# Eight experts' feed-forward on one core: the stores of seven experts regrouped into 8 KB runs

## The chip, the core and the metric

The kernel runs on one NeuronCore of a Trainium2 chip. The metric is the device time of one execution in microseconds (us): 180.81 us, the median of 4 runs between 180.52 and 181.08 us. One further execution was taken with the hardware profiler; it took 181.58 us, and all rows of the profile come from it.

## The reference

Eight experts each have their own 256 tokens of 512 values and their own two weight matrices. All arrays are float32.

```python
n_experts, capacity, hidden, expert_hidden = 8, 256, 512, 2048
# x (8, 256, 512), w1 (8, 512, 2048), w2 (8, 2048, 512)
h = np.matmul(x, w1)
h = np.maximum(h, 0)
return np.matmul(h, w2).astype(np.float32)     # (8, 256, 512)
```

## The kernel before

Data comes in through one queue of GpSimd (POOL), queue q0 of the profile, which also casts float32 to bfloat16 on the way. Ahead of it SyncE (SP) loads a first quarter of x, `x_head`, on its own queue q1. Then q0 carries, in the order of the code: the rest of x; w1 and w2 of experts 0 and 1; w1 and w2 of experts 2 and 3; w1 of 4 and 5; w2 of 4; w2 of 5; w1 and w2 of 6; w1 of 7; w2 of 7 in two halves. The list `loads` holds the twelve weight loads. Four slots of SBUF (`w1_sb`, `w2_sb`, `NS = 4`) hold weights, so a load waits until the expert that used its slot four places earlier is done. x is put in slot 2 of `w2_sb` first, so the load of w2 of experts 2 and 3 also waits until x has been transposed.

TensorE (PE) first transposes x in a loop of four rounds. Each round fills two PSUM tiles, `xt_ps`, which VectorE (DVE) and ScalarE (ACT) copy to `xT` (`copy_xt`, line 194). Then a loop runs over the eight experts: 64 matmuls into `h_ps`, with the ReLU on ACT (line 225, into `hT`), and 32 matmuls into two tiles `o_ps` of 128 tokens each. DVE copies these into `out_sb` (line 211); of the last expert ACT copies the second (line 231). Semaphores `c_w1` and `c_w2`, which SP raises as each load lands (line 138), let PE go on; `c_o` tells PE that an `o_ps` tile has been copied away, and PE waits for it at the last hidden matmul of each half of the next expert.

Every partition of `out_sb` holds two neighbouring tokens of each expert. Thus a partition's piece of an expert is 4 KB that is contiguous in the output too. Experts 0 to 6 go out with one DMA from POOL (line 187, called "the bulk store" below). It follows the last load in q0. A tiny store of 16 times 64 bytes (line 175) stands in the queue between the two halves of w2 of expert 7, and the bulk store is not issued before it has landed:

```python
pool.wait_ge(s_event, 4)        # DVE has copied expert 6
pool.wait_ge(d_pool, 32)        # x and the tiny store have landed
pool.dma_start(
    out_v[:, :E - 1, :], out_sb[:, :E - 1].rearrange("p e m h -> p e (m h)")
).then_inc(d_pool, 16)
```

The last expert's 512 KB go out with a DMA from SP on q1 (line 140, "the last store"), after the last two copies of `o_ps`. At the end POOL waits for the bulk store and then for the last store, and the engines meet at a barrier.

In this kernel each weight slot has a semaphore of its own, so POOL may issue as many loads ahead as there are free slots.

Of the kernel before, what the change touches and what calls it, by code (L numbers as in the profile page):

```python
# [8 lines left out]
FP32 = mybir.dt.float32  # L9
# [7 lines left out]
def kernel(  # L17
# [8 lines left out]
    P = 128  # L26
    E, C, H = x.shape
    F = w1.shape[2]
    MC = C // P
# [3 lines left out]
    R = E * C // P  # L33

    HEAD = 4

    NS = 4
# [8 lines left out]

    x_v = x.rearrange("e (pp r) k -> (e pp) (r k)", r=R)
    w1_v = w1.rearrange("e (p ko) n -> p e (ko n)", ko=K1)  # L50
    w2_v = w2.rearrange("e (p h j) n -> p e h (j n)", h=2, j=JH)
    out_v = out.rearrange("e (p mo) k -> p e (mo k)", mo=MC)


    places, free = {}, FIRST_FREE
# [1 line left out]
    def allot(name, shape, dtype):  # L57
        nonlocal free
        places[name] = free
        t = nc.alloc_sbuf_tensor_at(name, shape, dtype, offset=free)  # L60
        free += math.prod(shape[1:]) * mybir.dt.size(dtype)
        return t


    out_sb = allot("out_sb", [P, E, MC, H], FP32)
    w1_sb = allot("w1_sb", [P, NS, K1 * F], BF16)
    w2_sb = allot("w2_sb", [P, NS, K2 * H], BF16)
    xT = allot("xT", [P, K1, MC, E * P], BF16)
# [4 lines left out]
    x_sb = w2_sb[:, 2, :]  # L73
    X_AT = W2_AT + 2 * K2 * H * 2

    xt_ps = [nc.alloc_psum_tensor(f"xt_ps{i}", [P, R // MC, P], BF16) for i in range(MC)]
    h_ps = [nc.alloc_psum_tensor(f"h_ps{i}", [P, GJ * C], FP32) for i in range(UG)]
    o_ps = [nc.alloc_psum_tensor(f"o_ps{i}", [P, H], FP32) for i in range(MC)]

    def sem(name):  # L80
        return tc.alloc_semaphore(name)

    d_w = {
        (w, i): sem(f"d_w{w}_{i}")
        for w, slots in [(1, (0, 2, 3)), (2, (0, 1, 2, 3))]
        for i in slots
    }
    d_half, d_pool, d_last = sem("d_half"), sem("d_pool"), sem("d_last")  # L90


    s_event = sem("s_event")
    s_pe, v_last = sem("s_pe"), sem("v_last")

    def after_transposes(n):
        return s_pe, n

    def after_hidden(e, groups):
        return s_pe, K1 * MC + e * (NG + MC) + groups  # L100

    def after_outputs(e, halves):
        return s_pe, K1 * MC + e * (NG + MC) + NG + halves
# [10 lines left out]
    loads = []  # L114
# [3 lines left out]
    for e in range(6, E - 1):  # L118
        loads += [(1, (e,), 0, 2), (2, (e,), 0, 2)]
    loads += [(1, (E - 1,), 0, 2), (2, (E - 1,), 0, 1), (2, (E - 1,), 1, 1)]  # L120
    landed, counts = [], {}
    for w, es, h, _ in loads:
        s = d_half if h else d_w[w, es[0] % NS]
        counts[id(s)] = counts.get(id(s), 0) + 16
        landed.append((s, counts[id(s)]))

# [4 lines left out]
    with tc.tile_critical(no_gpsimd_drain=True):  # L133

        sp = nc.sync
        for i, (w, es, h, n) in enumerate(loads):
            sp.wait_ge(*landed[i])
            sp.sem_inc((c_w1, c_w2)[w - 1], n * len(es) if w == 2 else len(es))
        sp.wait_ge(v_last, MC)
        sp.dma_start(  # L140
            out_v[:, E - 1, :], out_sb[:, E - 1].rearrange("p m h -> p (m h)")
        ).then_inc(d_last, 16)


        pool = nc.gpsimd
        pool.dma_start(x_sb[:, HEAD * H:], x_v[:, HEAD * H:]).then_inc(d_pool, 16)  # L146
        pool.memset(identity[:], 0.0).then_inc(s_event)  # L147
        pool.wait_ge(s_event, 1)

# [1 line left out]
            out=identity[:],  # L151
# [7 lines left out]
        for i, (w, es, h, n) in enumerate(loads):  # L159


            old = es[-1] - NS
            if w == 2 and 2 in es:
                tc.wait_critical_data_deps()
                pool.wait_ge(*after_transposes(K1 * MC))
            if old >= 0 and h == 0:
                if w == 1:
                    pool.wait_ge(*after_hidden(old, NG))
                else:
                    pool.wait_ge(*after_outputs(old, MC))  # L170
            if i == len(loads) - 1:


                pool.wait_ge(s_event, 3)
                pool.dma_start(  # L175
                    out_v[:16, 0, :16], out_sb[:16, 0, 0, :16]
                ).then_inc(d_pool, 16)
            e, ne, at_slot = es[0], len(es), es[0] % NS
            if w == 2:
                src = w2_v[:, e:e + ne, h:h + n, :].rearrange("p e h n -> p e (h n)")  # L180
                dst = w2_sb[:, at_slot:at_slot + ne, h * JH * H:(h + n) * JH * H]
            else:
                src, dst = w1_v[:, e:e + ne, :], w1_sb[:, at_slot:at_slot + ne, :]
            pool.dma_start(dst, src).then_inc(landed[i][0], 16)  # L184
        pool.wait_ge(s_event, 4)
        pool.wait_ge(d_pool, 32)
        pool.dma_start(  # L187
            out_v[:, :E - 1, :], out_sb[:, :E - 1].rearrange("p e m h -> p e (m h)")
        ).then_inc(d_pool, 16)

        def copy_xt(copy, ko, m):
            return copy(  # L194
                xT[:, ko, m].rearrange("k (ep r2) -> k ep r2", r2=R // MC),
                xt_ps[m][:].rearrange("k r2 ep -> k ep r2"),
            )


        dve = nc.vector  # L200
        dve.sem_inc(c_xt[0], 1)
        for ko in range(K1):
            dve.wait_ge(*after_transposes(ko * MC + 1))
            copy_xt(dve.tensor_copy, ko, 0).then_inc(c_xt[0])
        dve.sem_inc(c_o, MC)
        for e in range(E):
            for m in range(MC):
                if e == E - 1 and m == 1:
                    break
                dve.wait_ge(*after_outputs(e, m + 1))  # L210
                cp = dve.tensor_copy(out_sb[:, e, m, :], o_ps[m][:])  # L211
                cp.then_inc(v_last if e == E - 1 else c_o)
            if e in (4, E - 2):
                dve.drain().then_inc(s_event)  # L214


        act = nc.scalar
        act.sem_inc(c_xt[1], 1)
        for ko in range(K1):
            act.wait_ge(*after_transposes(ko * MC + 2))  # L220
            copy_xt(act.copy, ko, 1).then_inc(c_xt[1])
# [6 lines left out]
                    mybir.ActivationFunctionType.Relu,  # L228
                ).then_inc(c_h)
        act.wait_ge(*after_outputs(E - 1, MC))  # L230
        act.copy(out_sb[:, E - 1, 1, :], o_ps[1][:]).then_inc(v_last)  # L231

# [1 line left out]
        pe = nc.tensor  # L236
# [45 lines left out]
        def last_column(step):  # L282

            return (P - 1) * step * 2
# [25 lines left out]
                t.then_inc(s_pe)  # L310

        pe.wait_ge(s_event, 2)
        pe.wait_ge(d_pool, 16)
        x_first = X_AT + last_column(K1)
        pe.reg_mov(reg["x"], x_first)
        loop("transposes", reg["x"], x_first + K1 * 2, transposes)
# [116 lines left out]


        pool.drain()
        pool.wait_ge(d_pool, 48).then_inc(s_event)
        pool.wait_ge(d_last, 16).then_inc(s_event)


# [28 lines left out]
```

## Time and profile before

| what | value |
|---|---|
| median of 4 runs | 180.81 us (180.52 to 181.08) |
| the profiled execution: time, span | 181.58 us, 179.8 us |
| PE, ACT, DVE, POOL busy | 127.1, 38.7, 15.8, 10.2 us |
| q0: packets, bytes, share of the 16 DMA engines' span | 3456, 38.80 MB, 96.8% |
| q1: the same | 288, 1.57 MB, 2.3% |
| HBM read and written | 71.30 MB, 4.20 MB |
| bulk store: size, issue, time from issue to landing | 3584 KB, 164.63 us, 12.9 us |
| last store: the same | 512 KB, 175.59 us, 3.2 us |
| first and last wait of SP for a load (line 138) passed at | 33.1 us, 168.8 us |

The span runs from the first to the last instruction; the time of the execution is longer by 1.8 us that lie around it. The bytes of a queue are counted at the destination, where a weight has 2 bytes; 4 bytes of it are read. A "DMA share" is the mean busy share of the core's 16 DMA engines.

### The profile page before, as it was taken

What the parts mean: (1) busy time and instruction counts of PE and PEld (TensorE: products, weight loads), DVE (VectorE), ACT (ScalarE), POOL (GpSimd) and SP (SyncE); (2) the same over time, 40 slices, a digit from 0 to 9 for tenths busy, and PEclk for the clock granted to TensorE, in tenths of its full rate; (3) what the DMA queues carried; (4) which work ended last, traced back from release to release, by engine and by line L of the source; (5) the groups of instructions that cost most, each with busy time, mean ns of one, the idle gap of its engine ahead of it and who ended that gap; (6) DMA issues with size and microseconds to landing.
All of it is one profiled execution on the core that took longest, in us unless ns stands there. A gap on an engine that the chain in (4) does not pass through costs nothing. (4 is left out here: it accounts for less than half of the span.)

```text
span 179.8 us, 2088 instructions
## 1 busy us (share of the span) xinstructions
PE 127.1 (71%) x824; PEld 89.9 (50%) x832; DVE 15.8 (9%) x20; ACT 38.7 (21%) x38; POOL 10.2 (6%) x21
## 2 busy tenths in 40 slices
PE   0006630593029999994069999999999999869990
PEld 0006530493013696594024884894794695349630
DVE  0202520000000200110000200200200200200010
ACT  0202420044000044044000260242052063004400
POOL 6100010000000002001000100100100000002000
PEclk9999999999756999999759999999999999978999
DMA  5998999999899999989999998999999899899994
GB/s 213 236 236 186 233 230 197 215 233 230 179 233 233 197 211 233 230 179 233 233 200 208 233 230 179 233 233 200 208 233 230 179 233 233 184 222 206 379 420 167
DMA packets 3744, 40.37 MB, mean 225 GB/s; under 512 B 288, under 2 KB 288, under 8 KB 1312
## 3 DMA queue, kind: packets, MB, share of 16 engines
q0 software_dynamic: 3456, 38.80, 96.8%
q1 hardware_dynamic: 288, 1.57, 2.3%
HBM read 71.30 MB, written 4.20 MB: 420 GB/s over the span
## 5 line engine op out<-in xcount | busy, mean ns | idle before, releaser
L264 PE MATMUL o_ps<-w_sb,hT 128*128 x248 | 59.6, 395 | 19.5 <-PEq L239 18.7
L264 PE MATMUL h_ps<-xT,w_sb 128*128 x512 | 61.5, 282 | 11.8 <-PEq L239 11.8
L264 PEld LDWEIGHTS h_ps<-xT,w_sb 128*128 x512 | 58.1, 146 | 16.1 <-issue 12.7
L225 ACT ACTIVATE hT<-h_ps 128x1024 bf16<-128x1024 f32 x32 | 32.7, 1023 | 111.2 <-PE h_ps L264 111.2
L264 PEld LDWEIGHTS o_ps<-w_sb,hT 128*128 128x128 bf16 x256 | 25.4, 101 | 51.1 <-issue 24.6
L211 DVE COPY out_sb<-o_ps 128x512 f32<-128x512 f32 x15 | 9.7, 686 | 141.2 <-PE o_ps L264 141.2
L264 PE MATMUL xt_ps<-identity,w_sb 128*128 128x128 bf16 x64 | 7.6, 312 | 16.5 <-PEq L239 16.5
L264 PEld LDWEIGHTS xt_ps<-identity,w_sb 128*128 x64 | 6.5, 147 | 17.3 <-issue 17.3
L184 POOL DMA_DIRECT2D w_sb<-in_w_dram x12 | 7.4, 616 | 105.5 <-PE h_ps L264 57.4
L194 ACT COPY xT<-xt_ps 128x1024 bf16<-128x1024 bf16 x4 | 4.0, 1012 | 12.8 <-PE xt_ps L264 12.8
L194 DVE COPY xT<-xt_ps 128x1024 bf16<-128x1024 bf16 x4 | 4.9, 1224 | 12.8 <-PE xt_ps L264 12.8
L187 POOL DMA_DIRECT2D out_dram<-out_sb x1 | 1.0, 962 | 33.9 <-DMA out_dram<-out_sb 33.9
L194 ACT ACT_TABLE_LOAD x1 | 1.3, 1283 | 7.0 <-DVE w_sb L132 7.0
L231 ACT COPY out_sb<-o_ps 128x512 f32<-128x512 f32 x1 | 0.6, 585 | 5.9 <-PE o_ps L264 5.9
L132 DVE CAST w_sb<-x_head 128x2048 bf16<-128x2048 f32 x1 | 1.2, 1228 | 5.6 <-DMA x_head<-in_x_dram 5.6
L175 POOL DMA_DIRECT2D out_dram<-out_sb x1 | 0.5, 509 | 14.7 <-DVEq L214 14.7
L146 POOL DMA_DIRECT2D w_sb<-in_x_dram x1 | 0.7, 679 | 0.8 <-POOLq L452 0.8
L150 POOL TENSOR_SCALAR_AFFINE_SELECT identity<-identity 128x128 bf16<-128x128 bf16 x1 | 0.3, 283 | 0.2 <-POOL identity L147 0.2
L147 POOL MEMSET identity<- 128x128 bf16 x1 | 0.2, 223 | 0.0
L452 POOL MEMSET const-float32-0.0<- 128x1 f32 x1 | 0.1, 93 | 0.2 <-issue 0.2
L452 POOL MEMSET const-bfloat16-1.0<- 128x1 bf16 x1 | 0.1, 95 | 0.0
L452 POOL MEMSET const-uint8-127<- 128x1 uint8 x1 | 0.1, 95 | 0.0
(1 smaller groups left out, 0.1 us busy)
## 6 DMA issues: line engine op xcount, KB each, us to landing
w_sb<-in_w_dram POOLq DMA_DIRECT2D x5, 4096.0 KB, 48.9
w_sb<-in_w_dram POOLq DMA_DIRECT2D x5, 2048.0 KB, 51.5
out_dram<-out_sb POOLq DMA_DIRECT2D x1, 3584.0 KB, 12.9
w_sb<-in_w_dram POOLq DMA_DIRECT2D x2, 1024.0 KB, 44.1
w_sb<-in_x_dram POOLq DMA_DIRECT2D x1, 1536.0 KB, 12.5
x_head<-in_x_dram SPq DMA_DIRECT2D x1, 1024.0 KB, 4.8
out_dram<-out_sb SPq DMA_DIRECT2D x1, 512.0 KB, 3.2
out_dram<-out_sb POOLq DMA_DIRECT2D x1, 1.0 KB, 34.4
```

What stands on the lines that cost most here:

```text
L132: nc.vector.tensor_copy(x_sb[:, :HEAD * H], x_head[:])
L146: pool.dma_start(x_sb[:, HEAD * H:], x_v[:, HEAD * H:]).then_inc(d_pool, 16)
L150: pool.affine_select(out=identity[:], in_=identity[:], compare_op=mybir.AluOpType.not_equal, fill=1.0, base=0, pattern=[[-1, P]], channel_ ...
L175: pool.dma_start(out_v[:16, 0, :16], out_sb[:16, 0, 0, :16]).then_inc(d_pool, 16)
L184: pool.dma_start(dst, src).then_inc(landed[i][0], 16)
L187: pool.dma_start(out_v[:, :E - 1, :], out_sb[:, :E - 1].rearrange("p e m h -> p e (m h)")).then_inc(d_pool, 16)
L194: return copy(xT[:, ko, m].rearrange("k (ep r2) -> k ep r2", r2=R // MC), xt_ps[m][:].rearrange("k r2 ep -> k ep r2"),)
L211: cp = dve.tensor_copy(out_sb[:, e, m, :], o_ps[m][:])
L225: act.activation(hT[:, g * GJ:(g + 1) * GJ, :].rearrange("p a c -> p (a c)"), h_ps[g % UG][:], mybir.ActivationFunctionType.Relu,).then_in ...
L231: act.copy(out_sb[:, E - 1, 1, :], o_ps[1][:]).then_inc(v_last)
L264: return pe.add_instruction(inst)
L452: nc = _bacc.Bacc("TRN2", target_bir_lowering=False, num_devices=1)
```

## The change

The rows of the first six experts are dealt to partitions anew, so that a partition holds four neighbouring tokens of one expert: experts 2i and 2i+1 share tile i, the even one on partitions 0 to 63, the odd one on 64 to 127, and a run of 8 KB is contiguous in `out_sb` and in the output. Expert 6 keeps its 4 KB runs and lies with expert 7 in a new tile `last_sb`.

- The bulk store becomes two: three pairs in 8 KB runs (3 MB), issued once expert 5 has been copied and the tiny store has landed, then expert 6 (512 KB).
- The tiny store covers 16 partitions of experts 0, 2 and 4: 48 pieces of 64 bytes in place of 16.
- `copy_xt` makes three copies in place of one, eight times in all.
- The copies of `o_ps` for experts 0 to 5 become two of 64 partitions each, in place of one of 128.
- POOL's DMAs take three semaphores in turn (`d_pool`), and DMA i waits until DMA i-3 has landed, so at most three are under way.

```diff
-    out_v = out.rearrange("e (p mo) k -> p e (mo k)", mo=MC)
+    HP = P // 2
+    PAIRS = E // 2 - 1
+    out_pairs = out[:2 * PAIRS].rearrange("(i s) (q r) k -> s q i (r k)", s=2, r=2 * MC)
+    out_v = out.rearrange("e (p m) k -> p e (m k)", m=MC)
...
-    out_sb = allot("out_sb", [P, E, MC, H], FP32)
+    out_sb = allot("out_sb", [P, PAIRS, 2 * MC, H], FP32)
+    last_sb = allot("last_sb", [P, 2, MC, H], FP32)
...
-    d_half, d_pool, d_last = sem("d_half"), sem("d_pool"), sem("d_last")
+    d_pool, d_last = [sem(f"d_pool{i}") for i in range(3)], sem("d_last")
...
+    of_load = [i + 1 for i in range(len(loads) - 1)] + [len(loads) + 1]
+    small, bulk, bulk2 = len(loads), len(loads) + 2, len(loads) + 3
+
+    def landed(i):
+        return d_pool[i % 3], 16 * (i // 3 + 1)
...
+        def queue(i, dst, src):
+            if i >= 3:
+                pool.wait_ge(*landed(i - 3))
+            pool.dma_start(dst, src).then_inc(d_pool[i % 3], 16)
...
-                pool.dma_start(
-                    out_v[:16, 0, :16], out_sb[:16, 0, 0, :16]
-                ).then_inc(d_pool, 16)
+                queue(small, out_pairs[0, :16, :, :16], out_sb[:16, :, 0, :16])
...
-            pool.dma_start(dst, src).then_inc(landed[i][0], 16)
+            queue(of_load[i], dst, src)
+        pool.wait_ge(*landed(small))
         pool.wait_ge(s_event, 4)
-        pool.wait_ge(d_pool, 32)
-        pool.dma_start(
-            out_v[:, :E - 1, :], out_sb[:, :E - 1].rearrange("p e m h -> p e (m h)")
-        ).then_inc(d_pool, 16)
+        queue(bulk, out_pairs, out_sb[:].rearrange("p i r h -> p i (r h)"))
+        pool.wait_ge(s_event, 5)
+        queue(bulk2, out_v[:, E - 2, :], last_sb[:, 0].rearrange("p m h -> p (m h)"))
...
         def copy_xt(copy, ko, m):
+            EP = 2 * PAIRS
+            for t in range(2):
+                copy(
+                    xT[:, ko, m, :EP * P].rearrange(
+                        "k (e t pp r4) -> k t e pp r4", e=EP, t=2, r4=R // 4
+                    )[:, t],
+                    xt_ps[m][:, :, :EP * (P // E)].rearrange(
+                        "k (r4 t) (e pp) -> k t e pp r4", t=2, e=EP
+                    )[:, t],
+                )
             return copy(
...
+        def copy_out(copy, e, m):
+            if e >= 2 * PAIRS:
+                return copy(last_sb[:, e - 2 * PAIRS, m, :], o_ps[m][:])
+            i, s = divmod(e, 2)
+            for t in range(2):
+                inst = copy(
+                    out_sb[s * HP:(s + 1) * HP, i, t * MC + m, :],
+                    o_ps[m][t * HP:(t + 1) * HP, :],
+                )
+            return inst
...
-            if e in (4, E - 2):
+            if e in (4, E - 3, E - 2):
                 dve.drain().then_inc(s_event)
...
-        pool.wait_ge(d_pool, 48).then_inc(s_event)
+        for i in (bulk, bulk2):
+            pool.wait_ge(*landed(i)).then_inc(s_event)
```

More of the change, by code (lines that the diff above doesn't have):

```diff
@@ L81, in sem @@
         return tc.alloc_semaphore(name)
[L85 to L89, printed above, removed]
-    d_half, d_pool, d_last = sem("d_half"), sem("d_pool"), sem("d_last")
+    d_pool, d_last = [sem(f"d_pool{i}") for i in range(3)], sem("d_last")
     s_event = sem("s_event")
@@ L120 @@
     loads += [(1, (E - 1,), 0, 2), (2, (E - 1,), 0, 1), (2, (E - 1,), 1, 1)]
[L121 to L125, printed above, removed]
+    of_load = [i + 1 for i in range(len(loads) - 1)] + [len(loads) + 1]
+    small, bulk, bulk2 = len(loads), len(loads) + 2, len(loads) + 3
+    def landed(i):
+        return d_pool[i % 3], 16 * (i // 3 + 1)
     x_pool = ctx.enter_context(tc.tile_pool(name="x_pool", bufs=1))
@@ L136 @@
         for i, (w, es, h, n) in enumerate(loads):
-            sp.wait_ge(*landed[i])
+            sp.wait_ge(*landed(of_load[i]))
             sp.sem_inc((c_w1, c_w2)[w - 1], n * len(es) if w == 2 else len(es))
@@ L140 @@
         sp.dma_start(
-            out_v[:, E - 1, :], out_sb[:, E - 1].rearrange("p m h -> p (m h)")
+            out_v[:, E - 1, :], last_sb[:, 1].rearrange("p m h -> p (m h)")
         ).then_inc(d_last, 16)
         pool = nc.gpsimd
-        pool.dma_start(x_sb[:, HEAD * H:], x_v[:, HEAD * H:]).then_inc(d_pool, 16)
+        def queue(i, dst, src):
+            if i >= 3:
+                pool.wait_ge(*landed(i - 3))
+            pool.dma_start(dst, src).then_inc(d_pool[i % 3], 16)
+        queue(0, x_sb[:, HEAD * H:], x_v[:, HEAD * H:])
         pool.memset(identity[:], 0.0).then_inc(s_event)
@@ L183 @@
                 src, dst = w1_v[:, e:e + ne, :], w1_sb[:, at_slot:at_slot + ne, :]
-            pool.dma_start(dst, src).then_inc(landed[i][0], 16)
+            queue(of_load[i], dst, src)
+        pool.wait_ge(*landed(small))
         pool.wait_ge(s_event, 4)
-        pool.wait_ge(d_pool, 32)
-        pool.dma_start(
-            out_v[:, :E - 1, :], out_sb[:, :E - 1].rearrange("p e m h -> p e (m h)")
-        ).then_inc(d_pool, 16)
+        queue(bulk, out_pairs, out_sb[:].rearrange("p i r h -> p i (r h)"))
+        pool.wait_ge(s_event, 5)
+        queue(bulk2, out_v[:, E - 2, :], last_sb[:, 0].rearrange("p m h -> p (m h)"))
         def copy_xt(copy, ko, m):
+            EP = 2 * PAIRS
[8 more added lines that the diff above has]
+                )
             return copy(
-                xT[:, ko, m].rearrange("k (ep r2) -> k ep r2", r2=R // MC),
-                xt_ps[m][:].rearrange("k r2 ep -> k ep r2"),
-            )
+                xT[:, ko, m, EP * P:].rearrange("k (ep r2) -> k ep r2", r2=R // MC),
+                xt_ps[m][:, :, EP * (P // E):].rearrange("k r2 ep -> k ep r2"),
+            )
+        def copy_out(copy, e, m):
[8 more added lines that the diff above has]
+            return inst
         dve = nc.vector
@@ L210 @@
                 dve.wait_ge(*after_outputs(e, m + 1))
-                cp = dve.tensor_copy(out_sb[:, e, m, :], o_ps[m][:])
+                cp = copy_out(dve.tensor_copy, e, m)
                 cp.then_inc(v_last if e == E - 1 else c_o)
-            if e in (4, E - 2):
+            if e in (4, E - 3, E - 2):
                 dve.drain().then_inc(s_event)
@@ L230 @@
         act.wait_ge(*after_outputs(E - 1, MC))
-        act.copy(out_sb[:, E - 1, 1, :], o_ps[1][:]).then_inc(v_last)
+        copy_out(act.copy, E - 1, 1).then_inc(v_last)
         pe = nc.tensor
@@ L312 @@
         pe.wait_ge(s_event, 2)
-        pe.wait_ge(d_pool, 16)
+        pe.wait_ge(*landed(0))
         x_first = X_AT + last_column(K1)
```

## Prediction

> **What bounds the kernel now.** I read the table of engine DMA use first, then the chain that ended last, then the stretches at the end, then the waits of SP and POOL.
>
> ```profile
> DMA  5998999999899999989999998999999899899994
> q0 software_dynamic: 3456, 38.80, 96.8%
> q1 hardware_dynamic: 288, 1.57, 2.3%
> ```
>
> The 16 DMA engines are occupied for 96.8 + 2.3 = 99% of the span. No engine of the core comes near (PE 71%).
>
> ```profile
> 159.09 0.04 issue
> 159.13 8.86 PE h_ps L264 x64
> 167.99 0.26 PE o_ps L264
> 168.25 0.05 issue
> 168.30 6.65 PE o_ps L264 x30
> 174.96 0.02 issue
> 174.98 0.58 ACT out_sb L231
> ```
>
> In the chain of waits the last expert starts at 159.1, when w1 of expert 7 has landed (SP passes that wait at 159.0), and runs unbroken into the last store. This looks like a bound by PE. The stretches of the end, whose last columns are DMA share and GB/s, say more:
>
> ```profile
> 100.00:150.00 50.00, 49.73 (x352) 37.43 (x355) 5.01 (x8) 15.92 (x16) 2.64 (x5) 1.00 1.01 216
> 168.00:175.00 7.00, 6.89 (x31) 2.93 (x30) 0.24 (x1) 1.04 (x2) 0.00 (x0) 1.00 1.02 419
> 176.00:177.00 1.00, 0.00 (x0) 0.00 (x0) 0.00 (x0) 0.00 (x0) 0.00 (x0) 1.00 0.62 254
> 177.00:178.00 1.00, 0.00 (x0) 0.00 (x0) 0.00 (x0) 0.00 (x0) 0.00 (x0) 1.00 0.72 291
> 178.00:179.00 1.00, 0.00 (x0) 0.00 (x0) 0.00 (x0) 0.00 (x0) 0.00 (x0) 1.00 0.02 8
> ```
>
> The bulk store runs at 419 GB/s with every DMA engine busy until about 176, and in the last microsecond 8 GB/s are left: one engine alone still works. The trace's packet and landing records show it. On every load one of the 16 engines reports about 1 us after the rest: for w1 of experts 0 and 1 the first fourteen by 31.93, the fifteenth at 32.15, the last at 33.12. I call it the straggler. It ends its share of the bulk store at 177.14, only then starts its eight packets of the last store (the others began theirs at 176.43), ends them at 178.39, and this landing at 178.74 is the last event before the closing barrier. So the end is set by the total work of one DMA engine that is never idle; PE's chain has 177.14 - 176.43 = 0.71 us of slack against it.
>
> Where the straggler fell behind is in the records too: its first packet of x begins about 0.5 us after it finished `x_head`, while the others follow within 6 ns, and takes 1.804 us in place of 0.926. No other packet after 5 us is longer than its kind by more than 0.12 us.
>
> **The time base.** The profiled execution took 181.58 (span 179.8, 1.78 around it), 0.77 above the median of 180.81. I sum on the profiled one and carry the difference over to the median. What a measurement here can tell from no change is about 0.3%, 0.54 us.
>
> **8 KB runs.** In the bulk store 4 KB packets of one engine start every 155.5 ns. Packets of 8 KB exist in the trace only as the `x_head` load, in the other direction: every 306 ns. An engine now has 56 x 155.5 = 8.71 us of bulk store; after, 24 x 306 + 8 x 155.5 = 8.59. That is -0.12 us, all of it on the straggler and so on the end. Bounds for an 8 KB store packet: 301 ns, if it had no cost beyond the bytes that the 16 KB reads show (605.5 ns, hence about 150 per 4 KB), which gives -0.24; twice the 172 ns of the slowest kind of 4 KB packet, the first of each engine, which gives 24 x 33 ns = +0.79. I take 306: same size, same 16 engines. [...]
>
> **The tiny store.** Its packets take 24 ns, one per engine; now three, so +0.05 us, ahead of the second half of w2 of expert 7 and the bulk store. If they do not follow each other so closely, I bound it by the 0.18 us between the landing of the load before it (163.87) and its own (164.05). **The second bulk store** adds a completion record of 9 to 22 ns per engine: +0.02. It is issued beside the first's 7 us of transfer; a POOL issue takes 0.5 to 0.7 us.
>
> **Three DMAs in flight.** POOL now issues each DMA when the third before it has landed; behind a waiting POOL stand only its own later DMAs. SP's waits show landings at 33.1, 52.5, 71.9, 91.2, 110.5, 120.2, 130.0, 139.6, 149.3, 159.0, 163.9, 168.8. Example: w2 of expert 5 was issued at 76.3, now at about 91.8, but w1 of 4 and 5 and w2 of 4 lie ahead of it until 120. The tightest place is the second half of w2 of expert 7: issued at 130.1 before, now after the landing at 159.0. POOL needs 0.28 to 0.6 us from semaphore to issue and 0.55 for the issue, so 160.2. From the end of an issue to a first packet at most 1.35 us passed (bulk store: issue over at 165.59, first packet at 166.94, and that one followed a busy queue). So 161.5 at the latest, and the fastest engines finish the first half at 162.06, the straggler a microsecond later. No gap, 0.5 us to spare: 0. The bulk store itself waits for the same landing at 164.05 as before.
>
> **Copies.** 512 elements take DVE 690 ns, 1024 take 1224: 156 ns fixed, so three copies in place of one are +0.31 us; ACT alike (585, 1012). Four rounds: +1.3 us, or +2.5 if both engines' shares add up, and the transposes end at 25.7 to 26.9 in place of 24.4. The first hidden matmul waits for weights until 33.1, so this is covered by 6 us; w2 of experts 2 and 3, which waits for the transposes, has a queue filled until 52 ahead of it. The halved output copies: two of 690 ns for one, 1.38 us until the first `c_o` and 2.76 until the second. PE asks for them at the last matmul of each half, some 3.6 and 7.2 us after the outputs end: covered. Expert 6 keeps single copies and is done at 157.6. All 0; without cover each transfer of `o_ps` would cost 0.7 us, and even that only beyond the 0.71 us of slack.
>
> **Sum.** -0.12 + 0.05 + 0.02 = -0.05: 181.53 on the profiled execution, 180.76 on the median. I write 180.7.
>
> **Rivals.**
>
> *Faster: the straggler catches up.* Its 1.4 us are lost around 4.8 to 7.1, just as POOL has finished issuing three weight loads (2.81 to 4.99) on top of x. After the change the third of them, w1 of 2 and 3, waits until x has landed at 13.8. [...] The fifteenth engine then decides, 33.12 - 32.15 = 0.97 us earlier: 180.76 - 0.97 = 179.8. Half of that stays within 0.3%. Against it: the later issues of loads, from 24.4 to 130.1, caused no such stall, and nothing proves the cause. [...]
>
> *Slower: late issue itself stalls an engine.* [...] If the straggler loses there what it lost on x, 0.5 + 0.88 = 1.4 us, the end moves fully: 182.1. If another engine does, 1.4 - 0.97 = 0.4: 181.2. [...] Against it: the bulk store before was issued 2.3 us before its first packets and no packet but one (+28 ns) was long. The 344 ns bound of the 8 KB packets would end at 181.6.
>
> *The runs are cut to 4 KB again:* then nothing remains but +0.07, 180.9, within 0.3%. *PE late by over 0.71 us:* nothing found that would do it.
>
> **How the numbers follow.** Little changed 0.47, the straggler catching up by over 0.54 us 0.33, a stall at the late issue or slow 8 KB writes 0.20. The range reaches to 179.5 on the fast side, which takes in that rival with its 8 KB bound, and to 181.7 on the slow side, leaving out the full stall. For the likeliest case alone it is 180.3 to 181.2.
>
> **What would show it.** Right: POOL's line for the 8 KB store near 164.6, SP's last landing at 168.8 to 168.9, 425 to 430 GB/s while the 8 KB packets run, the last landing at 178.6 to 178.7, transposes over by 27. The fast rival: SP's first load wait passes near 32.2 in place of 33.1 and every later one too. The slow rival: the last load lands after 169.5, or GB/s falls between 161 and 164. I am wrong altogether if PE stops for `c_o`, or if a stretch of the middle falls below 216 GB/s.

## The result and the profile after

The changed kernel takes 180.92 us (median of 50 runs), the kernel before 180.57 us (74 runs); the ratio is 1.002 with a 95% interval of 1.0013 to 1.0026. So it is slower by 0.36 us. That is inside the 0.3% that the prediction called no change and inside its range, but the sum said -0.05 us and the interval excludes that: a small loss where a smaller gain was forecast.

Time and span must be read apart here. In 63 executions of the changed kernel the time is 1.95 us or more above the span, 2.00 us in the mean; in the 149 of the kernel before that ran beside the experiments it is 1.71 to 1.82 us, 1.76 in the mean. The mean span is 179.00 against 178.85 us. So 0.24 us of the loss lie outside the span, where the prediction did not look, and 0.1 to 0.15 us inside it (0.15 by the mean spans, 0.12 by the medians of the time).

The profiled execution of before on which the prediction rests was an odd one: 181.58 us, when 74 runs lie between 180.31 and 181.53. A second trace of the same kernel (the run e1_before below, 180.68 us) has no DMA engine that lands 1 us late: w1 of experts 0 and 1 lands by 32.17 us on fifteen engines and at 32.24 on the last. SP's waits for the loads, with their first and last start in us, show it. Of that second trace of before:

```profile
L138 SPq EVENT_SEMAPHORE  x1: 17/17/17, 32.3 to 32.3; - x1
L138 SPq EVENT_SEMAPHORE  x2: 17/17/17, 163.0 to 167.9; - x2
```

And of the changed kernel, where the line has become 143:

```profile
L143 SPq EVENT_SEMAPHORE  x1: 17/17/17, 32.2 to 32.2; - x1
L143 SPq EVENT_SEMAPHORE  x2: 17/17/17, 162.9 to 168.4; - x2
```

The loads run alike until 163; then the last one, the second half of w2 of expert 7, lands 0.5 us later than in the second trace of before. The chain of the changed kernel, cut at its ends, is the one of before, some 0.9 us earlier only because the straggler is missing:

```profile
158.12 0.04 issue
158.16 8.96 PE h_ps L295 x64
...
174.12 0.59 ACT last_sb L221
```

The windows of time at the end (window, PE, PEld, DVE, ACT, POOL, clock, DMA share, GB/s), first of the second trace of before:

```profile
100.00:150.00 50.00, 50.00 (x353) 37.06 (x352) 4.30 (x7) 16.38 (x16) 2.26 (x5) 1.00 1.01 215
168.00:175.00 7.00, 6.05 (x29) 2.55 (x26) 0.69 (x1) 0.74 (x2) 0.00 (x0) 1.00 1.02 422
177.00:178.00 1.00, 0.00 (x0) 0.00 (x0) 0.00 (x0) 0.00 (x0) 0.00 (x0) 1.00 0.10 37
178.00:179.00 1.00, 0.00 (x0) 0.00 (x0) 0.00 (x0) 0.00 (x0) 0.00 (x0) 1.00 0.00 0
```

Then of the changed kernel:

```profile
100.00:150.00 50.00, 49.55 (x346) 36.68 (x349) 9.75 (x15) 16.39 (x16) 2.67 (x5) 1.00 1.01 215
168.00:174.00 6.00, 6.00 (x29) 2.55 (x26) 0.10 (x1) 0.19 (x1) 0.00 (x0) 1.00 1.01 429
177.00:178.00 1.00, 0.00 (x0) 0.00 (x0) 0.00 (x0) 0.00 (x0) 0.00 (x0) 1.00 0.25 98
178.00:179.00 1.00, 0.00 (x0) 0.00 (x0) 0.00 (x0) 0.00 (x0) 0.00 (x0) 0.83 0.00 0
```

The middle is the same (215 GB/s in both, where the first trace of before had 216), the 8 KB packets move 429 GB/s in place of 422, and yet more is left to move after 177 (98 against 37). What was gained by the stores was lost before they began. The window from 163 to 167.3, in which the last load's packets run, shows where, of the second trace of before:

```profile
163.00:167.30 4.30, 4.30 (x40) 4.08 (x39) 0.00 (x0) 2.21 (x3) 0.96 (x1) 1.00 0.96 209
```

and of the changed kernel:

```profile
163.00:167.30 4.30, 4.30 (x38) 3.95 (x38) 0.00 (x0) 2.19 (x3) 1.34 (x2) 1.00 0.98 194
```

The DMA engines are as busy (0.96, 0.98) and move less. The packet records say how: in the changed kernel 21 of the last load's packets, between 165.18 and 166.38 us, take 684 to 1004 ns in place of 625, together 4.85 us or 303 ns per DMA engine. In the second trace of before it is 7 ns per engine. I call this the stretch: what the packets of the last load take above 625 ns each, divided by 16.

### The profile page after: what moved, and what is told of

It is laid out like the page before. It is cut to its first block, busy times and chain, and to the rows that moved or that the text cites. A ratio compares the mean times of both kernels' runs of the same rounds, so it can differ in the third digit from the quotient of the medians.

```text
span 179.2 us, 2129 instructions
## 1 busy us (share of the span) xinstructions
PE 126.7 (71%) x824; PEld 89.7 (50%) x832; DVE 25.2 (14%) x40; ACT 39.2 (22%) x46; POOL 10.6 (6%) x22
## 5 line engine op out<-in xcount | busy, mean ns | idle before, releaser
L224 DVE COPY out_sb<-o_ps 64x512 f32<-64x512 f32 x24 | 16.5, 689 | 103.2 <-PE o_ps L295 102.8
L206 ACT COPY xT<-xt_ps 128x384 bf16<-128x384 bf16 x8 | 3.4, 482 | 11.9 <-PE xt_ps L295 11.9
L221 DVE COPY last_sb<-o_ps 128x512 f32<-128x512 f32 x3 | 2.0, 688 | 28.9 <-PE o_ps L295 28.9
L206 DVE COPY xT<-xt_ps 128x384 bf16<-128x384 bf16 x8 | 4.1, 552 | 12.0 <-PE xt_ps L295 12.0
L221 ACT COPY last_sb<-o_ps 128x512 f32<-128x512 f32 x1 | 0.6, 586 | 5.9 <-PE o_ps L295 5.9
L214 DVE COPY xT<-xt_ps 128x256 bf16<-128x256 bf16 x4 | 1.7, 414 | 0.0
L214 ACT COPY xT<-xt_ps 128x256 bf16<-128x256 bf16 x4 | 1.6, 390 | 0.0
L155 POOL DMA_DIRECT2D out_dram<-last_sb x1 | 0.6, 574 | 0.0
```

The lines of the kernel that those rows point to most:

```text
L155: pool.dma_start(dst, src).then_inc(d_pool[i % 3], 16)
L206: copy(xT[:, ko, m, :EP * P].rearrange("k (e t pp r4) -> k t e pp r4", e=EP, t=2, r4=R // 4)[:, t], xt_ps[m][:, :, :EP * (P // E)].rearran ...
L214: return copy(xT[:, ko, m, EP * P:].rearrange("k (ep r2) -> k ep r2", r2=R // MC), xt_ps[m][:, :, EP * (P // E):].rearrange("k r2 ep -> k ...
L221: return copy(last_sb[:, e - 2 * PAIRS, m, :], o_ps[m][:])
L224: inst = copy(out_sb[s * HP:(s + 1) * HP, i, t * MC + m, :], o_ps[m][t * HP:(t + 1) * HP, :],)
```

## The experiments

Two questions: what lies outside the span, and what stretches the last load. Time, mean span, mean of time minus span, and the stretch per engine in the profiled execution of each kernel:

| kernel | time us | ratio (interval) | span | outside | stretch ns |
|---|---|---|---|---|---|
| e1_before | 180.60 | 1.0002 (0.9993 to 1.0011) | 178.87 | 1.76 | 7 |
| e1_after | 180.93 | 1.0018 (1.0009 to 1.0027) | 178.89 | 2.02 | 354 |
| e1_queue3 | 180.51 | 0.9996 (0.9987 to 1.0005) | 178.75 | 1.79 | 39 |
| e1_layout | 180.88 | 1.0016 (1.0007 to 1.0025) | 178.85 | 2.03 | 40 |
| e2_split | 180.61 | 1.0002 (0.9992 to 1.0012) | 178.87 | 1.78 | 10 |
| e2_xt3 | 180.69 | 1.0004 (0.9994 to 1.0013) | 178.76 | 1.91 | 31 |
| e2_dve20 | 180.62 | 1.0002 (0.9992 to 1.0011) | 178.88 | 1.78 | 26 |
| e2_act8 | 180.67 | 1.0007 (0.9997 to 1.0016) | 178.76 | 1.93 | 0 |
| e3_noact | 180.67 | 1.0016 (1.0001 to 1.0031) | 179.07 | 1.77 | 79 |
| e3_act24 | 180.62 | 1.0001 (0.9992 to 1.0010) | 178.89 | 1.77 | 0 |
| e3_both | 180.81 | 1.0010 (1.0001 to 1.0019) | 178.80 | 2.00 | 0 |
| e3_early | 180.96 | 1.0021 (1.0012 to 1.0030) | 179.22 | 1.75 | 577 |
| e4_pieces | 180.91 | 1.0015 (1.0005 to 1.0024) | 179.14 | 1.77 | 218 |
| e4_gap | 184.93 | 1.0220 (1.0197 to 1.0243) | 183.12 | 1.77 | 0 |
| e4_swap | 180.75 | 1.0007 (0.9998 to 1.0016) | 179.03 | 1.75 | 216 |
| e4_after16 | 180.94 | 1.0016 (1.0007 to 1.0026) | 178.99 | 2.03 | 57 |
| e5_late2 | 180.68 | 1.0006 (0.9997 to 1.0014) | 178.95 | 1.77 | 77 |
| e5_two | 180.58 | 1.0002 (0.9993 to 1.0010) | 178.89 | 1.76 | 28 |

**Both kernels once more.**

> The kernel before, unchanged, taken again: a second trace of it, and the spans of many executions. Theory A (the profiled execution of before held a rare straggling DMA engine): this trace has no engine that lands 1 us after the rest, the span is about 178.6 us, and the loads of the last microseconds (the second half of w2 of expert 7) run at 606 ns a packet to the end. Theory B (the straggler is normal and the change removed it): the last of 16 landings is again 1 us behind. If part of the +0.35 us lies outside the span, time minus span is about 1.8 us here against 2.0 us in the changed kernel.

> The changed kernel, unchanged, taken again. Theory A (the late issue of the stores disturbs the last load): the packets of the second half of w2 of expert 7 are stretched again to 700 to 1000 ns for about a microsecond before the stores begin, and the time is +0.35 us against before. Theory C (the stretch was chance): no stretch in this trace, and +0.35 us all the same.

Theory A on the straggler holds: e1_before has none. The stretch is back in the second trace of the changed kernel (28 packets, 354 ns per engine), and the rate from 163 to 167.3 is low again, of e1_after:

```profile
163.00:167.30 4.30, 4.30 (x32) 3.15 (x31) 0.00 (x0) 2.05 (x2) 1.34 (x2) 1.00 1.03 198
```

And time minus span is 1.76 against 2.02 us, on one chip and in one set of runs. The spans differ little: 178.89 us of e1_after is 0.08 above the 178.82 of the 33 executions of before beside it.

**The queue alone, the layout alone.** e1_queue3 is the kernel before with these lines:

```diff
+        def queue(i, dst, src):
+            if i >= 3:
+                pool.wait_ge(*landed(i - 3))
+            pool.dma_start(dst, src).then_inc(d_pool[i % 3], 16)
```

e1_layout is the changed kernel without them: each weight slot has its own semaphore again.

> The kernel before with the three semaphores and the wait for the third DMA before alone; stores in 4 KB runs, tiny store and copies as before. Theory A (late issue of the last load and the stores costs): +0.3 us or more. Theory D (the 8 KB layout or its second store costs): 0.0 us within 0.1. If code length outside the span costs, +0.1 us at most.

> The changed kernel with the semaphores and the early issue of before: 8 KB runs, second bulk store, wider tiny store and the split copies stay. Theory A (late issue costs): -0.1 to 0.0 us against before. Theory D (layout, second store or split copies cost): +0.3 us, and the stretch of the last load's packets is there.

Three DMAs in flight cost nothing (0.9996), the rest costs all: the layout, the second store, the wider tiny store and the split copies give +0.31 us. Of that 0.26 us are outside the span. In this trace of e1_layout the stretch is small (40 ns). The last store lands at 177.71 us, in e1_before at 177.85; the nine traces with the old mapping of tokens to partitions and no straggler go from 177.65 to 177.91, so that alone shows no gain. The mean over the 16 landings of that store says it better: 177.40 us in e1_layout, 177.47 to 177.53 in those nine traces, so a gain of some 0.1 us is there.

**What lies outside the span.** The change adds 21 instructions to DVE and 8 to ACT. Four kernels add such instructions to the kernel before.

```diff
 e2_split, for experts 0 to 5
-                cp = dve.tensor_copy(out_sb[:, e, m, :], o_ps[m][:])
+                for half_of in ([slice(0, P)] if e >= E - 2 else [slice(0, P // 2), slice(P // 2, P)]):
+                    cp = dve.tensor_copy(out_sb[half_of, e, m, :], o_ps[m][half_of, :])
 e2_xt3, in copy_xt
+            for a, z in [(0, 48), (48, 96), (96, 128)]:
+                inst = copy(xT_of(ko, m)[:, a:z], xt_ps_of(m)[:, a:z])
 e2_dve20
+        for i in range(20):
+            dve.tensor_copy(pad[:, 0, i:i + 1], xT[:, 0, 0, :1])
 e2_act8
+        for i in range(8):
+            act.copy(pad[:, 1, i:i + 1], xT[:, 0, 1, :1])
```

(`xT_of` and `xt_ps_of` stand for the two views that `copy_xt` has.)

> The kernel before with the output copies of experts 0 to 5 halved (12 more DVE instructions, same places, 4 KB runs). Theory E (the time outside the span, 1.77 us before and 2.0 us after, grows with the number of instructions on DVE or ACT): time minus span rises, to 2.0 us if the DVE copies of the output are what does it; span unchanged at 178.8. Theory F (it is the 8 KB store or the third DMA that adds to what lies outside): 1.77 us as before, time 180.6.

> The kernel before with copy_xt in three pieces, same layout (8 more instructions on DVE, 8 on ACT). Theory E with ACT: time minus span rises to 2.0 us; with DVE alone it rises less than with 12 more, or not. Theory F: 1.77 us.

> The kernel before with 20 one-element copies on DVE into a scratch tile, after the last copy of xT, where DVE is idle. Theory E with DVE: time minus span about 2.0 us, span unchanged. Theory E with ACT, or theory F: 1.77 us, time 180.6.

> The kernel before with 8 one-element copies on ACT into a scratch tile, after the last copy of xT, where ACT is idle. Theory E with ACT: time minus span about 2.0 us, span unchanged. Theory E with DVE, or theory F: 1.77 us, time 180.6.

More instructions on DVE alone change nothing (1.78, 1.78). Eight more on ACT, idle work on one element each, put 0.17 us outside the span (1.93), and the three-piece copies, which add eight to ACT too, 0.15 us (1.91). So the stores are not needed for it. The spans of these two are 0.09 us shorter in the mean than those of the kernel before beside them, so that their time rises by less than 0.1 us, which their intervals do not tell from no change. The next three test the count of instructions as a rule.

```diff
 e3_noact, on the changed kernel
+            dve.wait_ge(*after_transposes(ko * MC + 2))
+            copy_xt(dve.tensor_copy, ko, 1).then_inc(c_xt[1])
-        for ko in range(K1):
-            act.wait_ge(*after_transposes(ko * MC + 2))
-            copy_xt(act.copy, ko, 1).then_inc(c_xt[1])
 e3_act24: the loop of e2_act8 with range(24)
 e3_both: e2_act8, and the loop of e2_dve20 with range(21)
```

> The changed kernel with all copies of copy_xt on DVE, so that ACT has 4 fewer instructions than in the kernel before instead of 8 more. Theory E (ACT's instruction count sets the time outside the span): time minus span falls from 2.02 to 1.77 us and the time from 180.9 to 180.65 us. Theory E' (ACT is 0.16 us of it and DVE's 21 more instructions the other 0.09 us): 1.85 us, 180.75 us. Theory F (the stores do it): 2.02 us, 180.9 us. The transposes end later, near 29 us, under the cover of the wait for weights until 32.2.

> The kernel before with 24 one-element copies on ACT after the last copy of xT. If the time outside the span grows by the instruction (0.16 us for 8, 20 ns each): 2.25 us, time 181.1. If it is a step that the eighth or an earlier instruction crosses: 1.93 us, time 180.7.

> The kernel before with 8 one-element copies on ACT and 21 on DVE, as many as the change adds to each. Theory E' (both counts add): time minus span 2.02 us, the whole of what the changed kernel has. Theory E (ACT alone): 1.93 us, and the remaining 0.09 us is from something else in the change.

e3_both, the kernel before with nothing but 29 idle copies, has 2.00 us outside the span and +0.2 us in time: as much as the changed kernel has outside. e3_noact, the changed kernel with all twelve of ACT's copies of xT given to DVE, has 1.77 (1.72 to 1.82 in its 12 executions). So the instruction mix on ACT and DVE makes the 0.24 us, and without ACT's copies it is gone. (In the time of e3_noact this shows as a median of 180.67 us; its ratio of 1.0016 does not show it, since one execution took 182.09.) But it doesn't grow with the number: 24 on ACT give 1.77. The last of this series adds 16 to ACT in the changed kernel.

```diff
 e4_after16, on the changed kernel
+        for i in range(16):
+            act.copy(pad[:, 1, i:i + 1], xT[:, 0, 1, :1])
```

> The changed kernel with 16 more one-element copies on ACT after the last copy of xT, 24 more than the kernel before in all. Where ACT's program ends decides what lies outside the span (+8 gave 1.93 us, +24 gave 1.77 us): time minus span falls from 2.02 us to 1.77 to 1.85 us, and the changed kernel becomes faster by added instructions, 180.7 us. If the number of instructions on all engines decides: 2.02 us or more, 180.95 us.

That theory falls: 2.03 us. The place where ACT's program ends is not the rule either, or not alone. The trace shows part of it: the last semaphore update after the span comes 2.02 to 2.03 us behind the span's end in the changed kernel and in all kernels with eight more on ACT (e1_layout, e2_xt3, e2_act8, e3_both), and at 1.91 us in all others, e3_act24 and e4_after16 among them. So where the later update is there, 0.12 us come after the last instruction; the rest no record shows, and in e4_after16, which has 2.03 us with its last update at 1.91, nothing recorded shows any of it.

**What stretches the last load.** First, the stores issued early, so that POOL does nothing at that time.

```diff
 e3_early, on e1_layout with the copies of e3_noact
-                pool.wait_ge(s_event, 3)
-                pool.dma_start(
-                    out_pairs[0, :16, :, :16], out_sb[:16, :, 0, :16]
-                ).then_inc(d_pool, 16)
...
         pool.wait_ge(s_event, 4)
-        pool.wait_ge(d_pool, 32)
```

> The changed kernel with the semaphores of before, all copies of copy_xt on DVE, and no tiny store: the 8 KB store is issued once expert 5 is copied, long before the last load ends, the 512 KB store of expert 6 once that is copied. If the stretch of the last load's packets comes from the stores' issue at 163.5 to 164.9, it is gone, the last load lands spread over less than 0.5 us, the span is 178.7 us and with 1.77 us outside the time 180.45, below the kernel before. If the stretch has another cause, it is there again, at 165.2 to 166.6.

POOL's issues in this kernel are long over, as its instructions in order of time show:

```profile
145.31 0.75 POOL L190 DMA_DIRECT2D out_dram<-out_sb  x1 [29.78 <-DVEq L245]
157.87 0.57 POOL L194 DMA_DIRECT2D out_dram<-last_sb  x1 [11.80 <-DVEq L245]
```

and the stretch is the worst of all, 577 ns per engine, at the same place, as the rate from 163 to 167.3 shows:

```profile
163.00:167.30 4.30, 4.30 (x32) 3.08 (x31) 0.00 (x0) 2.05 (x2) 0.00 (x0) 1.00 0.98 177
```

So neither late issue nor the tiny store makes it. Three kernels, all on e3_noact, change what stands behind the load.

```diff
 e4_pieces: the 8 KB store as two DMAs of 4 KB pieces
+        for t in range(2):
+            queue(
+                bulk + t,
+                out_pairs[:, :, :, t * MC * H:(t + 1) * MC * H],
+                out_sb[:, :, t * MC:(t + 1) * MC].rearrange("p i r h -> p i (r h)"),
+            )
 e4_gap: ahead of queue(bulk, ...)
+        pool.wait_ge(*landed(of_load[-1]))
 e4_swap: expert 6 first
+        queue(bulk, out_v[:, E - 2, :], last_sb[:, 0].rearrange("p m h -> p (m h)"))
+        queue(bulk2, out_pairs, out_sb[:].rearrange("p i r h -> p i (r h)"))
```

> The changed kernel, with the copies of copy_xt all on DVE, and its 8 KB store cut into two DMAs that carry the first and the second 4 KB of each run: the same tiles and places, packets of 4 KB. Theory G (8 KB packets queued behind the last load stretch that load's packets): no stretch, the second half of w2 of expert 7 lands by 167.8 on all engines, the stores take 8.71 us again, and the span is 178.8 us as before the change. Theory H (the stretch comes from the tiles' places or from something else at that time): stretched packets of 700 us to 1000 ns at 165.2 to 166.4 all the same.

> The changed kernel, with the copies of copy_xt all on DVE, and the 8 KB store not issued before the last load has landed, so that nothing stands behind that load in the queue. Theory G: no packet of the last load is stretched, it lands spread over less than 0.5 us by 167.8; the stores start some 1.5 to 2 us later, which the end pays. Theory H: the stretch is there again at 165.2 to 166.4.

> The changed kernel, with the copies of copy_xt all on DVE, and the two stores in the other order: expert 6 in 4 KB runs stands right behind the last load, the 8 KB runs follow. Theory G: no stretch, the last load lands by 167.7, the stores keep the gain of 8 KB packets of 0.1 us, span 178.7 us, time 180.45 to 180.5, a little below the kernel before. Theory H: span 178.9 us, time 180.65 as with the order of the change.

With nothing behind it, the last load is not stretched in any packet:

```profile
163.00:167.30 4.30, 4.30 (x36) 3.50 (x35) 0.00 (x0) 2.57 (x3) 0.00 (x0) 1.00 1.04 217
```

In this one trace, then, there is no stretch without the queued stores, as theory G has it. Its other half falls: packets of 4 KB stretch it as well (e4_pieces 218, e4_swap 216 ns). The gap costs 4.3 us, more than the 1.5 to 2 expected. In the trace (of the longest of its four executions, 185.63 us) the first store packet starts at 170.36 in place of 166.94 in e1_before, which is 3.4 us, and the span ends 1.9 us after the last landing in place of 1.1; the second bulk store now lands after the last store, at 181.92 against 181.74.

Last, the number of stores behind the load.

```diff
 e5_late2, on e3_noact
         pool.wait_ge(s_event, 5)
+        pool.wait_ge(*landed(of_load[-1]))
         queue(bulk2, out_v[:, E - 2, :], last_sb[:, 0].rearrange("p m h -> p (m h)"))
 e5_two, on the kernel before
-            out_v[:, :E - 1, :], out_sb[:, :E - 1].rearrange("p e m h -> p e (m h)")
+            out_v[:, :E - 2, :], out_sb[:, :E - 2].rearrange("p e m h -> p e (m h)")
         ).then_inc(d_pool, 16)
+        pool.dma_start(
+            out_v[:, E - 2, :], out_sb[:, E - 2].rearrange("p m h -> p (m h)")
+        ).then_inc(d_more, 16)
```

> The changed kernel, with the copies of copy_xt all on DVE, and the store of expert 6 not issued before the last load has landed; the 8 KB store stands behind that load alone, and its 7 us of transfer cover the later issue. Theory I (a second store in the queue behind the last load causes the stretch): under 50 ns of stretch per DMA engine, span 178.7 us, time 180.45 us, below the kernel before. Theory J (the mapping of tokens to partitions, or chance, causes it): 80 to 350 ns per engine as with both stores, span 178.9 us, time 180.65 us.

> The kernel before with its bulk store cut into two DMAs, experts 0 to 5 and expert 6, both in 4 KB runs and issued one after the other. Theory I: the last load's packets are stretched by 100 ns or more per DMA engine, span 178.9 to 179.0 us, time 180.7 us. Theory J: under 40 ns per engine and 180.6 us as before.

Theory I falls: a second store in the kernel before doesn't stretch (28 ns), and delaying it in e3_noact, which has 79, leaves 77 ns. The rate of e5_two is that of before:

```profile
163.00:167.30 4.30, 4.30 (x39) 3.94 (x38) 0.00 (x0) 2.19 (x3) 1.40 (x2) 1.00 0.97 210
```

What stays is the new mapping of tokens to partitions. Ten traces with the old mapping (the first one of before among them) have 0 to 39 ns per engine, nine with the new one and a store behind the load have 40 to 577. The two groups only just do not overlap, so the mapping is the likeliest condition and not a shown cause. Which property of it would do it, the places in HBM or in SBUF, no run separates. The stretch varies from execution to execution (303 and 354 ns in two traces of the changed kernel), so single traces size it badly.

That the stretch reaches the end of the kernel, the landings of the last store show. Their mean over the 16 engines is 177.40 us in e1_layout with 40 ns of stretch, 177.46 in e5_late2 (77), 177.52 in e3_noact (79), 177.58 in e4_swap (216), 177.64 and 177.80 in the two traces of the changed kernel (303 and 354), and 177.92 in e3_early (577). e4_pieces, whose 4 KB packets lack the gain, has 177.71 (218); e4_after16, in whose trace the loads before were already 0.4 us late, has 177.81 (57).

No version beat the kernel before by more than its interval. e1_queue3 had the lowest median, 180.51 us, at 0.9996 (0.9987 to 1.0005).

## Why the prediction was wrong, point by point

- **The time base.** The step that failed first. The time around the span, in its words "span 179.8, 1.78 around it", was carried over as fixed without a reason, and the change's 29 extra instructions were priced by what covers them inside the span. They are covered there, but 0.24 us appear outside it: e3_both makes that with idle copies alone, e3_noact takes it away. Why such copies count there stays open. That 180.92 us lies inside the stated range owes nothing to the sum: neither this nor the stretch is a term of it.
- **The straggler.** The prediction rested on it as the end of the kernel. It belonged to one execution. The main claim survives without it: in e1_before all DMA engines work until about 177 (DMA share 0.99 from 176 to 177) and PE's chain is not the end. That the gain of the 8 KB runs, which was put on the straggler, still holds is because all 16 engines carry it: from the 16 landings of the last load to the 16 of POOL's last store, both in order of time, there are 8.60 to 8.70 us in the profiled execution of the changed kernel, and 8.69 to 8.88 in the first trace of before. What cost the straggler its time on x no run shows.
- **8 KB runs, -0.12.** Right in mechanism and size. From the first engine's landing of the last load to its landing of expert 6's data the stores take 176.01 - 167.39 = 8.62 us, in e1_before 176.03 - 167.30 = 8.73; 8.59 and 8.71 were forecast. The packets take 309 ns, as those of `x_head`, where two of 4 KB take 318 (159 each, in the same trace). With the runs of a partition 1 MiB apart in the output the changed kernel moves 429 GB/s, the second trace of before, with 512 KiB, 422.
- **The tiny store, +0.05.** Mis-sized: the three pieces travel in one packet of 192 bytes that takes 28 ns in place of 24.
- **"No gap" at the hand-over.** The queue never ran dry, as said (DMA share 0.98 from 163 to 167.3). But the bulk store was priced at 0 since it "waits for the same landing at 164.05 as before", which missed that the load ahead of it is itself stretched: 303 and 354 ns per engine in two traces of the changed kernel. This is the second failed step; it turns the -0.1 us of the stores into +0.1 to +0.15 us of span.
- **Three in flight, 0.** Right: 0.9996.
- **Copies, 0 on the path.** Right. These groups of the changed kernel, from its page, show the prices:

```profile
L224 DVE COPY out_sb<-o_ps 64x512 f32<-64x512 f32 x24 | 16.5, 689 | 103.2 <-PE o_ps L295 102.8
L221 DVE COPY last_sb<-o_ps 128x512 f32<-128x512 f32 x3 | 2.0, 688 | 28.9 <-PE o_ps L295 28.9
L206 DVE COPY xT<-xt_ps 128x384 bf16<-128x384 bf16 x8 | 4.1, 552 | 12.0 <-PE xt_ps L295 12.0
L214 DVE COPY xT<-xt_ps 128x256 bf16<-128x256 bf16 x4 | 1.7, 414 | 0.0
```

Three pieces take 2 x 552 + 414 = 1518 ns where one took 1224, +0.29 us (0.31 forecast). A copy of 64 partitions takes 689 ns, no less than one of 128 (688). The transposes suffered less than forecast: PE's wait between two rounds grew from 0.73 to 0.86 us, and the last copy of xT ended at 24.69 us in place of 24.27 in e1_before, +0.4 where +1.3 was the least forecast. The wait for weights until 32.3 covers that, and PE has no wait for an output copy in its list.

- **The rivals.** The fast one, a straggler that catches up, had no straggler to work on. Its sign, a first load wait passed near 32.2, is there in the changed kernel, and at 32.3 in the unchanged e1_before too: it tells the absence of the straggler and no effect of the change. The slow one named the right place, the last load, and the wrong cause: e1_queue3 has its late issue with little stretch (39 ns), e3_early the stretch without late issue (577 ns).

## What to carry to other kernels

When a change is worth a tenth of a microsecond, look at the time around the span too: here 29 idle copies on ACT and DVE put 0.24 us there (e3_both, 2.00 against 1.76 us), and the 8 KB runs brought 0.11 (8.62 against 8.73). Take a second trace before building on a feature of one, above all when the profiled execution lies outside the range of the other runs. And when one DMA queue is the bound, price the transfer that stands ahead of a changed store as well as the store: here its packets slowed, by 303 and 354 ns per engine in two traces, with nothing of its own changed.

## What the runs showed of the hardware

- Time minus span depends on the instructions of ACT, and of DVE beside them, but not in proportion: 1.76 us in the kernel before, 1.93 with 8 more on ACT, 1.77 with 24 more, 2.00 with 8 more on ACT and 21 on DVE, 1.78 with 20 on DVE alone. With 8 more on ACT alone the span was 0.09 us shorter at the same time. The rule is open.
- A load's packets slowed from 625 to as much as 1209 ns while stores waited behind them in the same queue: 577 ns per engine in the trace with the most (e3_early), 0 ns in the one trace of the same mapping with nothing queued behind (e4_gap), and 0 to 39 ns with stores of the old mapping queued.
- Three 64-byte pieces for each DMA engine went as one packet of 192 bytes in 28 ns, in the profiled execution of the changed kernel; one piece of 64 bytes took 24 in that of before.
- In the first trace of before, the time that one DMA engine lost at the start stayed to the end: the straggler's lag was 1.0 us at 32 us and still 1.1 us at 169.
